# A hybrid encoder block on one core: four small changes to when background transfers and side work happen

## The chip, the cores and the metric

One Trainium2 chip, one of its cores. The metric is the time of one execution in device microseconds. A kernel is run several times; the median is compared.

## The reference, cut to what matters

One encoder layer on x (512 tokens, width 2048), all in float32:

```
h = rms_norm(x) ; proj = h @ w_in
  group A: 16 heads of chunked banded softmax attention with a relative bias
  group B: 4 heads of gated linear attention, RMSNorm per head, silu gate
x = x + concat(A, B) @ w_out
u = causal_conv3(rms_norm(x) @ w_ffn_up)         # 11264 columns
x = x + (gelu(u_gate) * u_val) @ w_ffn_down      # 5632 -> 2048
x = x + sigmoid(rms_norm(x) @ w_ple_gate) * (p @ w_ple_proj)
return rms_norm(x)
```

## The kernel before

**Arithmetic.** Activations lie transposed: features on the 128 partitions, 512 tokens in the free dimension. Every float32 product is made as three products of two parts: ScalarE copies an operand to its rounded high part (`hi`), VectorE subtracts to get the low part (`lo`), and TensorE does hi·hi, hi·lo and lo·hi. On top of that each large matrix product is done by a seven-product scheme on 2 x 2 blocks (Strassen-Winograd). The weight side needs the quarters L11, L12, L22 and four sums of quarters, S1 = L21 + L22, S2 = S1 + L11, S3 = L21 + L11, S4 = S2 + L12. The activation side needs seven operands, R11, R21, R22, N1, T3, N2, T4, made from four quarters of a pair of feature blocks.

**Units, steps, stages.** A unit is one block of output features; for each unit the seven products P1, P2, P6, P5, P7, P3, P4 run in this order, and one product of one unit is a *step*. The list `steps` runs over all stages in turn; `base[unit]` is the unit's first step. The first and the last two units of the later stages are interleaved, product by product (the *head* pair and the *last* pair). The stages:

- linear (units 16, 20/21, 17, 22/23, 18, 8, 9, 19; steps 0 to 69). 16 to 19 are the four heads of group B, 20 to 23 the values of group A in two pairs (14 steps each), 8 and 9 the first two blocks of the output gate;
- front (units 0 to 7, which are group A's heads by pairs, then the gate blocks 10 and 11; from step 70);
- embed: four steps, the product p @ w_ple_proj, 24 wide matmuls each; its results are evicted from PSUM by ScalarE (`pp_o`) and stored to memory (`ppd`) from ScalarE's queue;
- wo (out projection), up, dn0, dn1, dn2 (down projection in three chunks), pg (the embedding's gate).

**The main loop** goes over `steps`. `agenda[i]` is a list of (k, function) that are called at step i beside its product: those with k = 0 first, then the high part of the weight operand of step i + 2, then k = 1, then the low part, then the product, then those with k above 1. Instructions on TensorE, VectorE and ScalarE keep this order. DMA instructions do not: the framework orders each issuing queue (SP's, ScalarE's, GpSimd's) by a simulated run in which an instruction goes out once what it needs is ready. Only a DMA wrapped in `tc.keep_in_program_order` stays behind everything that was written for its queue before it. Once the order is fixed, a queue is strictly in order: an instruction that waits holds up all behind it.

**Weights.** A raw quarter is loaded by SP into a page of 128 x 1024 floats from a pool of free pages (`issue`, L429 for quarters `l`); S1 and S3 come as a load on SP (L433) and an accumulating DMA on GpSimd (L434) into the same page, both called `s` in the profile. A page is free again when its low part has been made.

**Sums in memory.** For the first two units of up, dn0, dn2 and pg all four sums are made in device memory instead (`memory_sums`, the kind `mem`): eight DMAs, memory to memory, of 512 KB (up), in this order: S1 = L21 (SP, L381), S1 += L22 (GpSimd, L384), S3 = L21 (SP), S2 = S1 (SP), S2 += L11, S3 += L11 (GpSimd), S4 = S2 (SP), S4 += L12 (GpSimd). In the profile those of up's two units are called `up0S` and `up8S`. `MEMORY` (L1140) says at which steps they are issued: for up from step 12 on, one each 6 steps (the two units one after the other, to step 102); for the others from the first step of the fifth unit of up on, one each 5 steps.

**The output gate.** A gate unit u = 8 + g multiplies silu(r) with a head's normed output `on`, which `load_heads` (L882, DMA at L885) loads into a page of ring `x` at step base + 3 (g = 0), 6, 3, 6. In linear and front the ring `x` has one page only; the value units' results (`vo`, stored to `vad`, L1083) and `tp` use the same one. Then `store_pair` (L266) makes the other operands N1, T3, N2, T4 in a `tp` page and stores all seven to memory, R11, R21 and R22 straight from the unit's own page `u` (`mix_R`), N and T from `tp` (`mix_N`, `mix_T`); all these DMAs are SP's (L264). The ring `u` has two pages there. Of gate block 11 nothing is stored: its operands stay in SBUF (`tails[1]`).

**Splits for wo.** The operands of wo are loaded and split from the end of front on; the last two feature blocks come from `tails` by `wo.split(op, 1, False, (0,))` and `(1,)`. For `(1,)` the steps are i0 + 8, 9, 10, 12, 15, 14, 15 in the order of the products, with i0 the base of unit 11: i0 + 7 to i0 + 10 are the embedding's four blocks, and the first step of wo is i0 + 11.

**Squares.** For the next RMSNorm, `squares` makes ScalarE square a unit's two halves into one buffer `sq`, and VectorE add each to `acc`. `after_norm` (wo and dn2) calls it from the third step after the unit's last one.

Of the kernel before, what the change touches and what calls it, by code (L numbers as in the profile page):

```python
# [43 lines left out]
def encoder_block(ctx: ExitStack, tc: tile.TileContext, A, out):  # L44
    nc = tc.nc
# [54 lines left out]
    def page(ring, name, dt=F32, shape=(P, 1024)):  # L100
        tags = rings[ring]
        i = counts.get(ring, 0)
        counts[ring] = i + 1
        tag = tags[i % len(tags)]
        return page_pool(tag).tile(list(shape), dt, tag=tag, name=name)
# [152 lines left out]
    def operand_scratch(name, kb):  # L258
        n = (min(4, kb), kb - 4)
        return {(op, g): dp.tile([P, n[g] * 256], F32, name=f"{name}_{op}{g}") for op in OPS for g in range(2)}  # L260

    def store_operand(xd, op, k, src):
        c = k % 4 * 256
        nc.sync.dma_start(xd[op, k // 4][:, c:c + 256], src)  # L264

    def store_pair(xd, k, a, b, t=None):  # L266

        t = (page("x", "tp") if t is None else t).rearrange("p (o t) -> p o t", o=4)
        a0, a1, b0, b1 = a[:, 0:256], a[:, 256:512], b[:, 0:256], b[:, 256:512]
        ops = dict(R11=a0, R21=b0, R22=b1, N1=t[:, 0, :], T3=t[:, 1, :], N2=t[:, 2, :], T4=t[:, 3, :])  # L270

        def store(*names):
            for op in names if xd else ():
                store_operand(xd, op, k, ops[op])

        store("R11", "R21", "R22")
        vec.tensor_tensor(ops["N1"], a0, a1, ALU.subtract)
        store("N1")
        vec.tensor_tensor(ops["T3"], b1, a1, ALU.subtract)
        store("T3")  # L280
        vec.scalar_tensor_tensor(ops["N2"], ops["N1"], -1.0, b1, ALU.mult, ALU.subtract)
        store("N2")
        vec.scalar_tensor_tensor(ops["T4"], ops["N2"], -1.0, b0, ALU.mult, ALU.subtract)
        store("T4")
        return ops
# [3 lines left out]
    def xtile(op, g, name, dt=F32R):  # L289
        pool = xa[0] if X_TAGS.index((op, g)) < 6 else xb[0]  # L290
        return pool.tile([P, 2, 1024], dt, tag=f"{op}{g}", name=name)

    mixd = operand_scratch("mix", 8)
# [79 lines left out]
    def memory_sums(unit):  # L373
        n = unit.stage.kb * P
        w = lambda q: unit.stage.weights(unit.u, q)
        for q in ("S1", "S2", "S3", "S4"):
            in_memory[unit, q] = dp.tile([P, n], F32, name=f"{unit.stage.name}{unit.u}{q}")
        S = lambda q: in_memory[unit, q]

        def first(q, src):  # L380
            tc.keep_in_program_order(nc.sync.dma_start(S(q), src, max_dma_last_dim=n))  # L381

        def added(q, src):
            tc.keep_in_program_order(nc.gpsimd.dma_start(S(q), src, accum_op=ALU.add, max_dma_last_dim=n))  # L384

        return [lambda: first("S1", w("L21")), lambda: added("S1", w("L22")), lambda: first("S3", w("L21")),
                lambda: first("S2", S("S1")), lambda: added("S2", w("L11")), lambda: added("S3", w("L11")),
                lambda: first("S4", S("S2")), lambda: added("S4", w("L12"))]
# [217 lines left out]
    def load_x(src, unit):  # L606
        unit.xs = page("c", "xs").rearrange("p (s t) -> p s t", s=2)
        nc.sync.dma_start(unit.xs, src[unit.u])

    def residual(dst, unit):  # L610
        vec.tensor_tensor(unit.xs, unit.o, unit.xs, ALU.add)
        nc.sync.dma_start(dst[unit.u], unit.xs)

    def squares(unit, at, c=slice(0, T)):

        def square(s):
            if unit.first and s == 0:
                act.activation(acc[:, c], unit.xs[:, s, c], AF.Square)
            else:
                sqt[unit, s] = tp.tile([P, T], F32, tag="sq", name="sq")[:, c]  # L620
                act.activation(sqt[unit, s], unit.xs[:, s, c], AF.Square)

        def add(s):
            if (unit, s) in sqt:
                vec.tensor_tensor(acc[:, c], acc[:, c], sqt[unit, s], ALU.add)

        return [(at + i, k, lambda f=f, s=s: f(s)) for i, k, f, s in ((0, 2, square, 0), (1, 1, add, 0), (1, 2, square, 1),
                                                                      (2, 1, add, 1))]
# [3 lines left out]
    def weighted(col, unit):  # L632
        m = unit.u
        for s in range(2):
            act.activation(unit.o[:, s, :], unit.xs[:, s, :], AF.Copy, scale=col[:, m + 8 * s:m + 8 * s + 1])
# [29 lines left out]
    def after_norm(dst, xd, col):  # L665
        def after(unit):
            if unit.last is not None:
                return [(1, 0, lambda: nc.sync.dma_start(dst[unit.u], unit.xs))] + squares(unit, 6 + unit.last * 2)
            return [(0, 1, lambda: residual(dst, unit)), (1, 2, lambda: weighted(col, unit)),
                    (2, 1, lambda: store_pair(xd, unit.u, unit.o[:, 0, :], unit.o[:, 1, :]))] + squares(unit, 3)  # L670
        return after

    def after_add(dst):
# [5 lines left out]
    def after_up(unit):  # L679
# [19 lines left out]
        def join():  # L699
            ci, k, second = unit.slot  # L700
            if second:
                store_pair(gd[ci], k, held[0], unit.c[:, 1, :])
            else:
                held[0] = unit.c[:, 1, :]
# [14 lines left out]
    def after_gate(unit):  # L719
# [9 lines left out]
    stages = [Stage("wo", list(range(8)), 8, mixd, blk2(A["w_out"]), after_norm(streams[1], h2d, nffn), "s3", "dma",  # L729
                    begin=lambda u: load_x(streams[0], u), begin_at=6, chained=True)]  # L730
# [151 lines left out]
    def load_heads(unit):  # L882
        g = unit.u - 8
        unit.M = {"on": page("x" if g < 3 else "c", "on").rearrange("p (s t) -> p s t", s=2)}
        nc.sync.dma_start(unit.M["on"], ond[g])  # L885

    def after_gates(unit):
        g, M = unit.u - 8, unit.M

        def times():  # L890
            vec.tensor_tensor(unit.o, unit.o, M["on"], ALU.mult)

        def pair():
            ops = store_pair(mixd if g < 3 else None, 3 + g, unit.o[:, 0, :], unit.o[:, 1, :])
            if g == 3:
                tails[1] = ops

        return [(0, 1, lambda: vec.tensor_tensor(unit.o, unit.o, rb2, ALU.mult)),
                (1 if g < 2 else 0, 1.5, lambda: act.activation(unit.o, unit.o, AF.Silu))] + (
                    [(4, 1, times), (5, 1, pair)] if g < 2 else [(1, 1, times), (1, 3, pair)] if g == 2 else  # L900
                    [(0, 3, times), (0, 4, pair)])
# [201 lines left out]
    front = Stage("in", [0, 1, 2, 3, 4, 5, 6, 7, 10, 11], 8, None, front_weights, front_after, "dma", "dma", single=True)  # L1103
# [26 lines left out]
    base = {}  # L1130
# [6 lines left out]
            need = [[(u, name) for name in (NEEDS[u.sums] if u.kind != "pp" else ("L11",))] for u in group]  # L1137
            wanted += [e for es in zip(*need) for e in es]

    MEMORY = ((lambda: 12, 6, (4,)), (lambda: base[stages[4].units[4]], 5, (5, 7, 8)))  # L1140
    agenda = [[] for _ in range(len(steps) + 60)]
    now = [0]
    for a, b in zip(stages[3:], stages[4:]):
        i0 = base[a.units[-1]]
        for n, p in enumerate(PLAIN):
            op = PRODUCTS[p][1]
            for g in range(2):
# [3 lines left out]
                at = 2 * n + (11 if g else 8)  # L1151
                if g and b.chained and op in ("R21", "T4"):
                    at = max(at, 14 if op == "R21" else 15)
# [3 lines left out]
    for st in (linear, front):  # L1157
        for u in st.units:
            if 16 <= u.u < 20:
                items = gla_head(u)  # L1160
                u.follow = lambda unit, items=items: items
                u.early()
            elif 8 <= u.u < 12:
                agenda[base[u] + (3, 6, 3, 6)[u.u - 8]].append((0, lambda u=u: load_heads(u)))

    i0 = base[front.units[-1]]
    for n, p in enumerate(PLAIN):
        op = PRODUCTS[p][1]
        for g in range(2):
            kept = (op, g) == ("T3", 1)  # L1170
            agenda[i0 + (13 if kept else n + 1 + g)].append((0, lambda op=op, g=g: wo.load(op, g)))
            agenda[i0 + (15 if kept else n + 5)].append((3, lambda op=op, g=g: wo.split(op, g, True, ())))
        at = (7, 7, 8, 9, 15, 10, 11)[n]
        agenda[i0 + at].append((3.5, lambda op=op: wo.split(op, 1, False, (0,))))
        at, k = ((8, 1), (9, 1), (10, 1), (12, 1), (15, 3.6), (14, 3), (15, 3.6))[n]
        agenda[i0 + at].append((k, lambda op=op: wo.split(op, 1, False, (1,))))

    def embedding_load(raw):
# [22 lines left out]
        aux_tags[:] = ["b6", "b7"]  # L1201
        banks.extend(("b4", "b5"))

    for b0, gap, heads in MEMORY:
        ops = [[op for u in stages[h].units[:2] for op in memory_sums(u)] for h in heads]
        for n, op in enumerate(sum(ops, [])):
            agenda[b0() + n * gap].append((0, op))

    agenda[base[front.units[7]] + 7 + 12].append((5, attention_done))
# [174 lines left out]
    for i, (unit, prod) in enumerate(steps[:-4]):  # L1384
# [17 lines left out]
        if i - len(steps) in EARLY:  # L1402
            p, op, g = EARLY[i - len(steps)]
            t = xtile(op, g, "last")
# [162 lines left out]
```

## Time and profile before

| | |
|---|---|
| median of 3 runs | 2234.06 us (2233.76 to 2234.48) |
| the profiled execution | 2231.0 us, span 2229.3 us, mean granted TensorE clock 0.994 |
| TensorE (PE) busy | 2192.5 us, 98% of the span |
| its weight loads (PEld) | 2146.3 us, 96%, beside the matmuls |
| VectorE (DVE) | 1905.9 us, 85% |
| ScalarE (ACT) | 1340.0 us, 60% |
| GpSimd (POOL) | 179.8 us, 8% |
| DMA | 550.83 MB, mean 247 GB/s |

How to read the rows of the trace: start in us from the span's start, duration in us, engine, line, operation, output<-inputs, count; in square brackets the idle time of the engine before it and what ended it. Nearly all lines read L64, since one wrapper issues them; go by tile names. SPq is SP's queue of DMA instructions: its duration is that of the issue and not of the transfer. `wsplit` is a weight operand's high and low part, `accA`, `accB`, `accC` are PSUM banks of the products, `u` is where a unit's result is gathered, `pat`, `eb`, `en`, `dd`, `pz` belong to a head of group B. Rows of waits: engine, what waited, for whom, us in total, times, longest. Rows of windows: the stretch, its length, then busy us and count of PE, PEld, DVE, ACT and POOL, the granted clock (1.00 is full), the DMA engines' busy share, GB/s. Rows of DMA: issues, size, median us from issue to landing.

### The profile page before, as it was taken

How to read it: one execution, taken by the hardware profiler on the slowest of the kernel's cores; microseconds unless marked ns; L12 is line 12 of the kernel's file. 1: busy time of each engine (PE TensorE's matmuls, PEld its weight loads, DVE VectorE, ACT ScalarE, POOL GpSimd, SP SyncE). 2: the span in 40 equal slices, each digit the busy share in tenths (PEclk: the TensorE clock that was granted, in tenths of full speed). 3: DMA queues.
4: the chain of work that ended last, by engine and by line, in shares of the span. 5: the costliest groups of instructions: out<-in, count | busy, mean ns of one | idle time of the engine just before them, and what ended most of it. 6: DMA issues, size and time to landing. Idle time of an engine off the chain costs nothing.

```text
span 2229.3 us, 46370 instructions
## 1 busy us (share of the span) xinstructions
PE 2192.5 (98%) x18588; PEld 2146.3 (96%) x18588; DVE 1905.9 (85%) x2616; ACT 1340.0 (60%) x2005; POOL 179.8 (8%) x212
## 2 busy tenths in 40 slices
PE   9999999999989999999999999999999999999997
PEld 7899899999989999999999999999999999999996
DVE  8476668999879898999889888888899798898987
ACT  9455455777765575555555555555574564666765
POOL 0010110000000001111111111111000100000000
PEclk9999999999999999999999999999999999999998
DMA  7478878876898988999999999998876977879996
GB/s 235 140 192 216 227 201 211 198 208 171 262 300 255 297 276 212 263 279 253 262 254 240 256 245 274 249 258 227 241 275 222 301 234 238 328 251 341 300 288 201
DMA packets 224553, 550.83 MB, mean 247 GB/s; under 512 B 21296, under 2 KB 100400, under 8 KB 224336
## 3 DMA queue, kind: packets, MB, share of 16 engines
q1 hardware_dynamic: 180560, 441.15, 57.2%
q0 software_dynamic: 40512, 101.46, 26.2%
q10 hardware_dynamic: 3264, 5.24, 0.6%
q8 instruction: 146, 2.39, 0.4%
q14 instruction: 71, 0.58, 0.1%
HBM read 474.37 MB, written 103.81 MB: 259 GB/s over the span
## 4 chain that ended last, share of the span: by engine, by line
PE 89%; DVE 6%; DMA 2%; ACT 2%; issue 1%; SPq 0%; ACTq 0%; DVEq 0%; POOLq 0%
PE accA L64 45%; PE accC L64 23%; PE accB L64 11%; DVE wsplit L64 2%; PE v L242 1%; PE v L243 1%; PE v L244 1%; PE py L64 1%; PE ptr L64 1%; PE psc L64 1%; DMA ppd<-pp_o 1%; DMA s<-in_w_blk 1%; PE pat L64 1%; PE po L64 1%; DVE u L64 1%
## 5 line engine op out<-in xcount | busy, mean ns | idle before, releaser
L64 DVE TENSOR_TENSOR wsplit<-l,wsplit 128x1024 fp32r<-128x1024 f32 (+1 forms) x462 | 554.8, 1202 | 119.2 <-ACT wsplit L64 118.5
L64 ACT ACTIVATE wsplit<-l 128x1024 fp32r<-128x1024 f32 (+1 forms) x462 | 481.2, 1042 | 280.6 <-PE accC L64 118.5
L64 DVE TENSOR_TENSOR wsplit<-s,wsplit 128x1024 fp32r<-128x1024 f32 (+1 forms) x267 | 320.3, 1201 | 69.9 <-ACT wsplit L64 69.5
L64 ACT ACTIVATE wsplit<-s 128x1024 fp32r<-128x1024 f32 (+1 forms) x267 | 277.1, 1038 | 59.1 <-PE accB L64 36.2
L64 ACT ACTIVATE u<-accA 128x256 f32<-128x256 f32 x302 | 114.3, 378 | 286.6 <-PE accA L64 277.3
L64 PE MATMUL accA<-up_T,wsplit 128*128 128x256 f32 x2112 | 253.3, 276 | 0.0
L64 PEld LDWEIGHTS accA<-up_T,wsplit 128*128 128x128 f32 x2112 | 245.7, 188 | 0.1
L64 DVE SCALAR_TENSOR_TENSOR cv<-u,cw,cv 128x511 f32<-128x511 f32 (+1 forms) x176 | 131.7, 748 | 3.1
L434 POOL DMA_DIRECT2D s<-in_w_up x84 | 74.4, 886 | 733.3 <-DMA s<-in_w_up 229.7
L64 PE MATMUL accA<-up_R,wsplit 128*128 128x256 f32 x1056 | 126.9, 276 | 0.0
L64 PE MATMUL accB<-up_R,wsplit 128*128 128x256 f32 x1056 | 126.5, 276 | 0.0
L64 PE MATMUL accC<-up_R,wsplit 128*128 128x256 f32 x1056 | 126.5, 276 | 0.0
L64 PE MATMUL accA<-up_N,wsplit 128*128 128x256 f32 x1056 | 126.5, 276 | 0.0
L64 PE MATMUL accC<-up_N,wsplit 128*128 128x256 f32 x1056 | 126.5, 276 | 0.0
L64 PE MATMUL accA<-dn_T,wsplit 128*128 128x256 f32 x1056 | 125.6, 276 | 0.2 <-DVE u L64 0.2
L64 PEld LDWEIGHTS accA<-up_R,wsplit 128*128 128x128 f32 x1056 | 122.9, 188 | 0.5 <-issue 0.5
L64 PEld LDWEIGHTS accB<-up_R,wsplit 128*128 128x128 f32 x1056 | 122.8, 188 | 0.0
L64 PEld LDWEIGHTS accC<-up_N,wsplit 128*128 128x128 f32 x1056 | 122.8, 188 | 0.0
L64 PEld LDWEIGHTS accA<-up_N,wsplit 128*128 128x128 f32 x1056 | 122.8, 188 | 0.0
L64 PEld LDWEIGHTS accC<-up_R,wsplit 128*128 128x128 f32 x1056 | 122.8, 188 | 0.0
L64 PEld LDWEIGHTS accA<-dn_T,wsplit 128*128 128x128 f32 x1056 | 122.4, 188 | 0.4 <-issue 0.4
L64 PE MATMUL accA<-in_T,wsplit 128*128 128x256 f32 x768 | 94.5, 279 | 2.4 <-ACT u L64 1.8
(345 smaller groups left out, 4235.7 us busy)
## 6 DMA issues: line engine op xcount, KB each, us to landing
l<-in_w_up SPq DMA_DIRECT2D x132, 512.0 KB, 5.4
s<-in_w_up SPq DMA_DIRECT2D x84, 512.0 KB, 5.3
s<-in_w_up POOLq DMA_DIRECT2D x84, 512.0 KB, 6.5
l<-in_w_dn SPq DMA_DIRECT2D x56, 448.0 KB, 5.6
l<-in_w_blk SPq DMA_DIRECT2D x48, 512.0 KB, 5.5
s<-in_w_blk SPq DMA_DIRECT2D x32, 512.0 KB, 4.5
s<-in_w_blk POOLq DMA_DIRECT2D x32, 512.0 KB, 7.4
l<-in_w_out SPq DMA_DIRECT2D x28, 512.0 KB, 5.1
```

The source lines that it names most:

```text
L64: ins = f(*args, **kw)
L242: nc.tensor.matmul(ps[t], x[:, 0, sl], wh, start=kt == 0, stop=False)
L243: nc.tensor.matmul(ps[t], x[:, 0, sl], wl, start=False, stop=False)
L244: nc.tensor.matmul(ps[t], x[:, 1, sl], wh, start=False, stop=kt == KD - 1)
L434: nc.gpsimd.dma_start(t, src("L22" if name == "S1" else "L11"), accum_op=ALU.add)
```

## The change

1. **Sums in memory.** Each unit has its own start and spacing. Up's first unit: from step 3, one each 4 steps (to step 31). Up's second unit: from the first step of front unit 1 (step 77), one each 5 steps (to 112). The 48 operations of dn0, dn2 and pg stay at the steps they had.
2. **Stores of the gate units.** For gate blocks 8 and 9 the stores of R11, R21 and R22 go on GpSimd's queue; those of N1, T3, N2 and T4 stay on SP's. `load_heads` of block 8 is called at step base + 5 instead of base + 3.
3. **Last pair's splits.** The three splits of `tails[1]` for the first three products come at i0 + 9, 10, 11 instead of i0 + 8, 9, 10.
4. **Squares.** For the second unit of a head pair (wo and dn2) they start one step later.

```diff
-    def store_operand(xd, op, k, src):
+    def store_operand(xd, op, k, src, queue=None):
         c = k % 4 * 256
-        nc.sync.dma_start(xd[op, k // 4][:, c:c + 256], src)
+        (queue or nc.sync).dma_start(xd[op, k // 4][:, c:c + 256], src)
...
-                store_operand(xd, op, k, ops[op])
+                store_operand(xd, op, k, ops[op], queue if op[0] == "R" else None)
...
-                    (2, 1, lambda: store_pair(xd, unit.u, unit.o[:, 0, :], unit.o[:, 1, :]))] + squares(unit, 3)
+                    (2, 1, lambda: store_pair(xd, unit.u, unit.o[:, 0, :], unit.o[:, 1, :]))] + squares(unit, 3 + (unit.head == 1))
...
-            ops = store_pair(mixd if g < 3 else None, 3 + g, unit.o[:, 0, :], unit.o[:, 1, :])
+            ops = store_pair(mixd if g < 3 else None, 3 + g, unit.o[:, 0, :], unit.o[:, 1, :], queue=nc.gpsimd if g < 2 else None)
...
-    MEMORY = ((lambda: 12, 6, (4,)), (lambda: base[stages[4].units[4]], 5, (5, 7, 8)))
+    MEMORY = [[(4, 0), lambda: 3, 4], [(4, 1), lambda: base[front.units[1]], 5]]
+    for n, (h, k) in enumerate(((5, 0), (5, 1), (7, 0), (7, 1), (8, 0), (8, 1))):
+        MEMORY.append([(h, k), lambda n=n: base[stages[4].units[4]] + 40 * n, 5])
...
-                agenda[base[u] + (3, 6, 3, 6)[u.u - 8]].append((0, lambda u=u: load_heads(u)))
+                agenda[base[u] + (5, 6, 3, 6)[u.u - 8]].append((0, lambda u=u: load_heads(u)))
...
-        at, k = ((8, 1), (9, 1), (10, 1), (12, 1), (15, 3.6), (14, 3), (15, 3.6))[n]
+        at, k = ((9, 1), (10, 1), (11, 1), (12, 1), (15, 3.6), (14, 3), (15, 3.6))[n]
...
-    for b0, gap, heads in MEMORY:
-        ops = [[op for u in stages[h].units[:2] for op in memory_sums(u)] for h in heads]
-        for n, op in enumerate(sum(ops, [])):
+    for (h, k), b0, gap in MEMORY:
+        for n, op in enumerate(memory_sums(stages[h].units[k])):
             agenda[b0() + n * gap].append((0, op))
```

More of the change, by code (lines that the diff above doesn't have):

```diff
@@ L260, in operand_scratch, with store_pair @@
         return {(op, g): dp.tile([P, n[g] * 256], F32, name=f"{name}_{op}{g}") for op in OPS for g in range(2)}
-    def store_operand(xd, op, k, src):
+    def store_operand(xd, op, k, src, queue=None):
         c = k % 4 * 256
-        nc.sync.dma_start(xd[op, k // 4][:, c:c + 256], src)
-    def store_pair(xd, k, a, b, t=None):
+        (queue or nc.sync).dma_start(xd[op, k // 4][:, c:c + 256], src)
+    def store_pair(xd, k, a, b, t=None, queue=None):
         t = (page("x", "tp") if t is None else t).rearrange("p (o t) -> p o t", o=4)
```

## The prediction

> **What bounds the kernel now.** First the page's busy shares, then TensorE's waits, then stretches of 40 us to find where it idles.
>
> ```profile
> PE 2192.5 (98%) x18588; PEld 2146.3 (96%) x18588; DVE 1905.9 (85%) x2616; ACT 1340.0 (60%) x2005; POOL 179.8 (8%) x212
> PE pp L64 <- ACT pp_o L64: 3.8, 1, 3.8
> PE accC L64 <- ACT u L64: 0.9, 1, 0.9
> 240.00:280.00 40.00, 35.33 (x263) 32.61 (x262) 23.27 (x28) 18.80 (x27) 3.68 (x5) 0.87 0.83 224
> 320.00:360.00 40.00, 35.82 (x295) 34.18 (x295) 29.22 (x39) 22.67 (x31) 4.55 (x5) 1.00 0.90 242
> ```
>
> TensorE is busy 2192.5 of 2229.3 us, and the change removes no matmul. What can be gained is its 36.8 us of idle time and whatever matmuls lose at a lowered clock. In 240 to 280 it idles 4.67 us and its mean granted clock is 0.87 (the last columns are clock, DMA share and GB/s); in 320 to 360 it idles 4.18 us at full clock. The wait of 3.8 us is in the embedding stage, the one of 0.9 us in the last down stage. I take these four places in turn, since each lies beside an edit.
>
> **Place A, 226 to 296 us: unit 18 and unit 8, the edit to the sums in memory.**
>
> ```profile
> 231.63 1.40 POOL L384 DMA_DIRECT2D up0S<-in_w_up  x1
> up0S<-in_w_up POOLq DMA_DIRECT2D x4, 512.0 KB, 13.9
> q0 software_dynamic: 1239, 1.67, 53.4%
> vad<-vo SPq DMA_DIRECT2D x8, 256.0 KB, 9.1
> SPq L885 <- DMA vad<-vo: 13.1, 2, 12.2
> 249.05 0.33 SPq L885 DMA_DIRECT2D on<-ond  x1
> 250.51 1.74 SPq L433 DMA_DIRECT2D s<-in_w_blk  x2
> 256.36 8.34 DMA s<-in_w_blk
> 264.79 1.22 DVE L64 TENSOR_TENSOR l<-l,s 128x1024 f32<-128x1024 f32 x1 [5.58 <-DMA s<-in_w_blk]
> 260.21 2.88 PE L64 MATMUL accA<-in_R,wsplit 128*128 128x256 f32 x24
> 267.28 1.46 PE L64 MATMUL accB<-in_R,wsplit 128*128 128x256 f32 x8 [2.38 <-DVE wsplit L64]
> 271.04 0.77 PE L64 MATMUL pat<-eb,en 128*128 128x128 f32 x2 [2.30 <-DVE eb L64]
> 271.00:275.60 4.60, 4.56 (x17) 3.23 (x17) 3.63 (x4) 0.00 (x0) 0.00 (x0) 0.50 0.44 130
> 295.94 3.30 PE L64 MATMUL accA<-in_R,wsplit 128*128 128x256 f32 x24
> ```
>
> Read it backwards. TensorE waits 2.38 us for a weight split and 2.30 us for `eb`; both stand on VectorE behind `l<-l,s`, which waited 5.58 us for an `s` load. That load's second half, GpSimd's accumulation, was issued at 256.36 and took 8.34 us; its first half left SP only at 250.51, because SP stood 12.2 us at `load_heads` (L885), whose page was still being read by a `vad` store. That store was in flight together with an accumulation for the up stage (231.63, the kind that takes 13.9 us to land), and GpSimd's queue took 53.4% of the DMA time in 232 to 250. After the change unit 0's eight operations are at steps 3 to 31 and unit 1's start at step 77, so nothing of this kind is left from step 32 to 76.
>
> The price: the 7 products from 260.21 to 295.94 took 35.73 us.
>
> ```profile
> 340.16 2.88 PE L64 MATMUL accA<-in_R,wsplit 128*128 128x256 f32 x24
> 368.08 3.30 PE L64 MATMUL accA<-in_R,wsplit 128*128 128x256 f32 x24
> ```
>
> The same work around the next head, 340.16 to 368.08, took 27.92 us, of which place B counts 0.5 as a wait: 27.4 clean. A loses 35.73 - 27.4 = 8.3 us: 4.7 of waits, the rest matmuls at a granted clock of 0.50 in 271.00 to 275.60. By the Trainium skill, page "TensorE: Matmul & The Clock Gate", part 1, the clock halves after an idle window of about 3.4 us. Neither wait here is that long alone, so read per wait it would grant no clock loss and A would be worth 4.7; the row of 0.50 decides, and I keep 8.3.
>
> Does the wait go entirely? For that, `s` must land 4.7 us before 256.36 + 8.34 = 264.7, by 260.0. SP reached `load_heads` at 249.05 - 12.2 = 236.9, just after the store, which so took 12.2 us or more. At the median of 9.1 (a median with such accumulations beside it) SP is free 3 us sooner, and the 8.34 us may shrink by 1 (estimate): 0.7 us of wait would be left, at full clock. With a store faster than that median nothing is left. So 7 to 8.3 us; I take 7.5. Moving `load_heads(8)` from step base+3 to base+5 I cost at nothing: at 249 us TensorE is at step 45, seven steps short of its place in the program, so its page sets its time and not its step; should it come behind the `s` loads, A only gets safer.
>
> **Place B, 308 to 350 us: unit 19, the stores on GpSimd's queue.**
>
> ```profile
> 239.91 2.89 PE L64 MATMUL accA<-in_R,wsplit 128*128 128x256 f32 x24
> 308.80 1.74 SPq L381 DMA_DIRECT2D up8S<-in_w_up  x1
> 311.40 1.67 SPq L264 DMA_DIRECT2D mix_R<-u  x3
> 315.39 2.88 PE L64 MATMUL accA<-in_R,wsplit 128*128 128x256 f32 x24
> 323.06 0.38 ACT L64 ACTIVATE u<-accA 128x256 f32<-128x256 f32 x1 [6.14 <-DMA mix_R<-u]
> 330.91 0.86 POOL L434 DMA_DIRECT2D s<-in_w_blk  x1 [21.43 <-DMA s<-in_w_blk]
> 345.60 0.39 ACT L64 ACTIVATE u<-accA 128x256 f32<-128x256 f32 x1 [3.17 <-DMA mix_R<-u]
> ```
>
> Unit 19's first eviction needs the `u` page that unit 8's three R stores still read. They leave SP from 311.40 behind a copy for the up stage (308.80), and ScalarE stands until 323.06, 6.14 us, with the next weight split behind it. Unit 19 lasts 340.16 - 315.39 = 24.77 us; the same seven products and `pz` of unit 18 take 260.21 - 239.91 = 20.30. That is 4.5 us, and 0.5 more at the next head's `pat` (the 3.17 us wait on unit 9's stores): 5.0 in all. After the change the copy is gone from SP, and the stores go on GpSimd, which idles 21.43 us before 330.91. Three issues at 0.86 us add 2.6 us to GpSimd, where no accumulation stands behind them until 330.91; the N and T stores on SP go 1.67 us earlier. Issued by 312, they land at 318 to 320 if they take 6 to 8 us (323.06 - 313.07 = 10 on SP); the eviction's product ends at 315.39 + 2.88 = 318.3. So 3.5 to 5.0 are gained; I take 4.2.
>
> The rule against it: page "DMA: Bandwidth & Descriptors" of the Trainium skill, section "Issuing engines are not separate DMA queues", says that transfers from any engine run on the same 16 DMA engines and that another issuer saves only issue time. By it the landing would stay at some 10 us; no run here shows yet which holds. That is a rival below.
>
> **Place D, embedding, 606 to 634 us: the last pair's splits.**
>
> ```profile
> 606.71 11.07 PE L64 MATMUL pp<-ps,wsplit 128*128 128x512 f32 x48
> 620.60 0.42 ACT L64 ACTIVATE wo_R<-u 128x256 fp32r<-128x256 f32 x1 [1.81 <-DVE u L64]
> 621.56 12.84 PE L64 MATMUL pp<-ps,wsplit 128*128 128x512 f32 x48 [3.78 <-ACT pp_o L64]
> 630.75 1.09 ACT L64 ACTIVATE pp_o<-pp 128x512 f32<-128x512 f32 x2 [1.92 <-DMA ppd<-pp_o]
> 634.24 5.62 PE L64 MATMUL accA<-wo_R,wsplit 128*128 128x256 f32 x48
> ```
>
> Half the work takes 11.07 us, all of it 27.53 (606.71 to 634.24): 5.4 lost. ScalarE stands 1.81 us at the R11 split of the last pair, then splits 0.42 us, before it evicts for the second block; with the split one block later these evictions start 2.2 us sooner. What is late next: the page that `ppd` still reads, which stops ScalarE at 630.75 whatever comes before, and ScalarE's full load as the out projection begins, where three splits now come one step nearer their use. Bounds 0 and 5.4 (if the clock stays up too); I take 1.5, nearer the 2.2 less that second stop.
>
> **Place E, second down-stage head: the squares.**
>
> ```profile
> 1961.98 0.63 ACT L64 ACTIVATE sq<-xs 128x512 f32<-128x512 f32 x1 [2.54 <-DVE acc L64]
> ```
>
> Two squares share one buffer, the second waits 2.54 us for VectorE's sum, and an eviction behind it costs TensorE the 0.9 us of the second row of waits above. A step later the buffer is free: 0.9 gained, bounds 0 and 1. The same edit in the out projection meets no wait of TensorE: 0.
>
> **What it adds: eight sums in steps 3 to 31.**
>
> ```profile
> 118.14 0.88 POOL L434 DMA_DIRECT2D s<-in_w_v_a  x1 [16.52 <-DMA s<-in_w_v_a]
> 126.86 1.23 DVE L64 TENSOR_TENSOR l<-l,s 128x1024 f32<-128x1024 f32 x1 [0.17 <-DMA s<-in_w_v_a]
> 129.56 0.46 PE L64 MATMUL pat<-eb,en 128*128 128x128 f32 x2
> 157.58 0.86 POOL L434 DMA_DIRECT2D s<-in_w_blk  x1 [17.71 <-DMA s<-in_w_blk]
> q1 hardware_dynamic: 180560, 441.15, 57.2%
> q0 software_dynamic: 40512, 101.46, 26.2%
> ```
>
> By the last two rows 0.52 MB costs the 16 DMA engines 1.5 us on q1 (57.2% of 2229.3 us over 441.15 MB) and 3.0 us on q0. The first copy, at step 3 (about 113 us), goes on SP just ahead of the loads that GpSimd waits for at 118.14. VectorE already waits 0.17 us for their sum at 126.86, and `pat` follows at 129.56 with hardly any slack: 1.5 us of delay can pass straight to TensorE. The next head's loads meet an extra accumulation of 3.0 us. Bounds 0 and 3.0 (twice 1.5); I take 1.5. On SP the copy S2<-S1 now follows the accumulation into S1 by 8 steps instead of 12; at 2.9 us a step (20.30 / 7) that is 23 us, against 13.9 to land, so 0, but see the second rival. Unit 1's eight operations, at steps 77 to 112, lie under attention, where TensorE waits for no load: 0. The other stages' 48 operations keep their steps.
>
> Sum: 7.5 + 4.2 + 1.5 + 0.9 - 1.5 = 12.6 us. The profiled execution took 2231.0 us (span 2229.3 and 1.7 around it), so 2218.4; the median of the runs is 3.06 above it: 2221.5, called 2222.
>
> **Rivals.** (1) The queue does not matter, as the skill's rule has it: only the copy that left SP (1.5 us) and 1.7 us of issue help, B gives 1.5: 2234.1 - 9.9 = 2224. For it: DMA share 0.90 in 320 to 360; against it: SP's queue holds loads ahead of the stores, GpSimd's does not. Chance 0.15.
> (2) Slower: S2<-S1 stands on SP waiting for the accumulation into S1, as `load_heads` does now. Place: step 15, about 151 us (`pat` at 129.56 is in step 9). It decides if that accumulation is queued on GpSimd behind the one of 157.58, which waits for unit 17's loads, so that it lands near 172: SP stands 21 us, and unit 17's second sum comes that late less the few us it has to spare, 18, with some 3.5 of lowered clock as in A. Less the 14.1 gained: +7, 2241. Chance 0.08.
> (3) The store before `load_heads` lands late without the sums too, A stays: gain 5.1, 2229. For it: the weight loads of that stretch and their own accumulations stay. Chance 0.14.
> (4) The loads of both early heads come so late that each `pat` wait trips the clock: 2 x 5.6 instead of 1.5, gain 3: 2231. Chance 0.07.
>
> **How the numbers follow.** The forecast has 0.56, at 2222. About 0.2% (4.5 us) is what a measurement of this kernel can tell from none. Faster: 0.56 + 0.15 + half of (3) = 0.77; same: half of (3) and (4), 0.14; slower, with (2) and a little for what I don't see: 0.09. Range: low end 2215.5, with A 8.3, B 5.0, D 4, E 1 and no cost (18.3); high end 2231, which takes in (3) and (4) and leaves out (2).
>
> **What would show it.** A: SP's wait at `load_heads` under 8 us, no TensorE wait between 250 and 285, clock 1.00 there. B: ScalarE's wait for `mix_R` under 2 us. D: TensorE's wait at `pp` near 1.6 us, perhaps a second one. E: no wait of accC for ACT. Cost: a new wait at `pat` near 130 and one head later. The forecast is wrong if TensorE idles anew between 100 and 240, or if A's wait stays.

## The result, and the profile after

| | before | after |
|---|---|---|
| median of 6 runs each, same chip | 2234.73 us | 2224.57 us (2221.58 to 2225.85) |
| ratio | | 0.995 [0.9939, 0.996] |
| profiled execution | 2231.0 us, span 2229.3 | 2225.11 us, span 2223.4 |
| mean granted clock | 0.994 | 0.997 |

The change gains 10.2 us by the medians; 12 were forecast. The page of the changed kernel, then its longest waits of TensorE beside the edits, then the two stretches of 40 us that the prediction began with (columns as there):

```profile
PE 2188.4 (98%) x18588; PEld 2141.1 (96%) x18588; DVE 1905.3 (86%) x2616; ACT 1339.5 (60%) x2005; POOL 182.9 (8%) x218
```

```profile
PE pp L64 <- ACT pp_o L64: 3.9, 3, 2.0
PE pat L64 <- DVE eb L64: 2.4, 3, 1.4
PE accA L64 <- ACT u L64: 2.2, 2, 1.9
```

```profile
240.00:280.00 40.00, 40.00 (x332) 38.20 (x331) 28.72 (x35) 21.99 (x32) 3.49 (x4) 1.00 0.81 217
320.00:360.00 40.00, 37.07 (x309) 35.62 (x308) 30.83 (x41) 21.82 (x31) 5.22 (x7) 1.00 0.71 187
```

Place A is clean: 40 of 40 us busy at full clock. Place B is not: 2.9 us idle are left. From the timeline, SP's waits and the loads of place A:

```profile
236.79 1.11 SPq L1083 DMA_DIRECT2D vad<-vo  x2
244.14 0.33 SPq L885 DMA_DIRECT2D on<-ond  x1
252.26 0.89 POOL L434 DMA_DIRECT2D s<-in_w_blk  x1 [18.29 <-DMA s<-in_w_blk]
262.03 2.88 PE L64 MATMUL accA<-in_R,wsplit 128*128 128x256 f32 x24
289.21 1.03 PE L64 MATMUL accA<-in_R,wsplit 128*128 128x256 f32 x4
```

```profile
SPq L885 <- DMA vad<-vo: 6.2, 1, 6.2
```

```profile
vad<-vo SPq DMA_DIRECT2D x4, 256.0 KB, 5.6
```

SP still stands at load_heads, in its old place in the queue, but 6.2 us instead of 12.2, since the `vad` stores land in 5.6 us; the same answer for before (226 to 262 us) has them at 8.9, beside two accumulations for the up stage of 15.3. From unit 8's first product to unit 9's are 27.18 us instead of 35.73.

**One profile is not enough here.** Each row of the next table is one execution; a cell is the difference of the start times of two first products (`accA<-in_R`, for the embedding `pp<-ps`) in its timeline. "Linear" goes from unit 16's at 103.35 to unit 18's at 239.91 (times of before), "unit 8" from 260.21 to 295.94, "B" from unit 19's to front unit 1's, 315.39 to 368.08, "attention" from there to the embedding, 606.71, "embedding" to the out projection's third unit, 675.25, "rest" to the end of the span. The last column is VectorE's wait for `s` loads under attention. The rows other than before and after are the experiments below.

| execution | linear | unit 8 | B | attention | embedding | rest | `s` waits |
|---|---|---|---|---|---|---|---|
| before | 136.56 | 35.73 | 52.69 | 238.63 | 68.54 | 1554.05 | 1.1 |
| before again | 137.68 | 36.96 | 53.15 | 241.08 | 69.46 | 1553.87 | 5.5 |
| sums as before | 138.62 | 36.61 | 52.89 | 240.32 | 67.93 | 1553.62 | 4.6 |
| sums only | 141.57 | 27.18 | 51.66 | 239.84 | 69.42 | 1553.76 | 2.3 |
| after | 138.46 | 27.18 | 51.80 | 242.15 | 67.87 | 1552.91 | 6.1 |
| load_heads as before | 137.30 | 27.18 | 51.75 | 242.24 | 67.95 | 1553.91 | 6.6 |
| stores on SP | 137.80 | 27.18 | 51.53 | 242.88 | 67.62 | 1552.61 | 7.2 |
| second unit in wo | 137.16 | 27.18 | 51.24 | 242.81 | 68.01 | 1555.22 | 7.1 |
| sums under attention | 137.27 | 27.18 | 50.84 | 243.53 | 68.55 | 1552.82 | 7.8 |
| stores from tp | 137.84 | 27.18 | 48.08 | 241.59 | 68.08 | 1552.85 | 4.5 |
| third page | 136.81 | 27.18 | 48.76 | 238.69 | 68.23 | 1552.78 | 0.2 |
| S1 first | 137.81 | 27.18 | 51.60 | 238.54 | 68.58 | 1553.39 | 0 |
| both | 140.97 | 27.16 | 48.25 | 238.58 | 67.94 | 1552.88 | 0 |
| both, linear too | 136.16 | 27.18 | 47.94 | 238.59 | 68.10 | 1553.19 | 0.8 |

### The profile page after: what moved, and what is told of

It is laid out like the page before. It is cut to its first block, busy times and chain, and to the rows that moved or that the text cites. A ratio compares the mean times of both kernels' runs of the same rounds, so it can differ in the third digit from the quotient of the medians.

```text
span 2223.4 us, 46366 instructions
## 1 busy us (share of the span) xinstructions
PE 2188.4 (98%) x18588; PEld 2141.1 (96%) x18588; DVE 1905.3 (86%) x2616; ACT 1339.5 (60%) x2005; POOL 182.9 (8%) x218
## 4 chain that ended last, share of the span: by engine, by line
PE 81%; DVE 9%; DMA 5%; ACT 2%; issue 2%; POOL 0%; ACTq 0%; DVEq 0%; SPq 0%; POOLq 0%
PE accA L64 42%; PE accC L64 21%; PE accB L64 11%; DVE wsplit L64 2%; DMA s<-in_w_blk 2%; PE v L244 1%; PE v L242 1%; PE v L243 1%; DVE sc L64 1%; DVE u L64 1%; DMA s<-in_w_v_a 1%; DVE s L64 1%; ACT wsplit L64 1%; PE po L64 1%; PE ptr L64 1%
```

## Experiments

All start from the changed kernel, unless said otherwise; ratios are to the kernel before, run beside them.

**1. Sums only** (the kernel before with part 1). Diff: the hunks on `MEMORY` and its loop.

> The kernel before with part 1 alone (both units' sums at their new steps). Theory, from the two traces: place A gains 8.5 (no wait of TensorE between 240 and 300), the two `pat` waits cost 1.9, place B gains 0.9 at most because a copy leaves SP, and 3.5 are lost between 380 and 605, since the second unit's sums move under attention. Sum about -4: 2230 to 2231 against some 2234.7. Rival: the 3.5 lost under attention are not the sums' doing; then -7.5, 2227. As I predicted it blind: -7.5 (A), +1.5 (early cost), -1.5 (B), 2227 too, but with no new waits under attention.

2225.2 us, 0.9963 [0.9951, 0.9975]: 8.6 us of the 10 are part 1's. The theory's 4 falls; the rival's 7.5 is near. Unit 8 takes 27.18 us. Attention lost nothing against the three executions with the old sums (239.84; they took 238.63 to 241.08), with 2.3 us of `s` waits. Linear took 141.57 us, 5 more than in the first profile of before, and here is why: the timeline has the wait at the second `pat`, and the window behind it the mean granted clock, 0.61.

```profile
200.08 0.46 PE L64 MATMUL pat<-eb,en 128*128 128x128 f32 x2 [1.39 <-DVE eb L64]
203.51 5.30 PE L64 MATMUL accB<-wsplit,in_R 128*128 128x256 f32 x24
```

```profile
200.00:207.50 7.50, 7.42 (x34) 6.39 (x35) 5.23 (x6) 0.51 (x1) 0.71 (x1) 0.61 0.70 123
```

The changed kernel's own trace, with a wait as long, keeps its clock in the same window:

```profile
129.86 0.46 PE L64 MATMUL pat<-eb,en 128*128 128x128 f32 x2 [0.48 <-DVE eb L64]
199.56 0.46 PE L64 MATMUL pat<-eb,en 128*128 128x128 f32 x2 [1.41 <-DVE eb L64]
```

```profile
200.00:207.50 7.50, 7.50 (x60) 6.87 (x60) 5.61 (x7) 1.55 (x2) 1.03 (x1) 1.00 0.68 129
```

So in these two executions a wait of 1.4 us cost 1.4, or 1.4 + 7.5 x 0.39 = 4.3.

**2. Sums as before** (part 1 undone).

```diff
-    MEMORY = [[(4, 0), lambda: 3, 4], [(4, 1), lambda: base[front.units[1]], 5]]
...
+    MEMORY = ((lambda: 12, 6, (4,)), (lambda: base[stages[4].units[4]], 5, (5, 7, 8)))
```

> The changed kernel with part 1 undone: sums at the steps they had, the other three parts stay. Theory: the embedding's splits give 1.0 and the squares 0.95, the stores on GpSimd nothing that can be seen: 2232 to 2233, and A's two waits with the granted clock near 0.5 stand at 267 and 271 as before. As predicted blind: 1.5 + 0.9 + 2.7 of B that I gave to the queue itself: 2229.6.

2233.56 us, 0.9998 [0.9989, 1.0006]: the other three parts together don't show in the time. The interval runs from 2.5 us gained to 1.3 lost, so a gain of 2 us is not excluded either. The two waits of place A are back, with the clock:

```profile
269.90 1.19 PE L64 MATMUL accB<-in_R,wsplit 128*128 128x256 f32 x8 [2.93 <-DVE wsplit L64]
273.66 0.77 PE L64 MATMUL pat<-eb,en 128*128 128x128 f32 x2 [2.57 <-DVE eb L64]
```

```profile
270.00:277.50 7.50, 4.93 (x22) 3.73 (x22) 7.21 (x9) 2.07 (x3) 0.00 (x0) 0.59 0.22 68
```

Its place B is instructive. The copy for the up stage is still on SP here, the stores are on GpSimd, and ScalarE's waits for the stores of unit 8 and then of unit 9 are 2.44 and 6.54 us, where before has 6.14 and 3.17:

```profile
312.76 1.65 POOL L264 DMA_DIRECT2D mix_R<-u  x3
323.44 0.38 ACT L64 ACTIVATE u<-accA 128x256 f32<-128x256 f32 x1 [2.44 <-DMA mix_R<-u]
349.34 0.38 ACT L64 ACTIVATE u<-accA 128x256 f32<-128x256 f32 x1 [6.54 <-DMA mix_R<-u]
```

So unit 19 was 2.6 us shorter (22.20 against 24.77), and front unit 0 took 30.69 us instead of 27.92; nothing was left.

**3. Stores on SP.**

```diff
-... queue=nc.gpsimd if g < 2 else None)
+... queue=None)
```

> The changed kernel with the R stores of gate blocks 8 and 9 on SP's queue again (the rest of the change stays). Theory (the queue does not matter, only what is in flight): the three stores of block 8 land some 11 us after issue on either queue, ScalarE waits 5 to 6 us for them, time within 1 us of the changed kernel, 2224 to 2226. Rival, my blind forecast: the queue itself is worth 2.7 of B's 4.2, so 2227 and a wait above 7 us; and unit 9's stores wait 3 us again.

2222.14 us, 0.995 [0.9938, 0.9962]; B takes 51.53 us against 51.80. With the copy gone, the queue makes no difference. First the stores and the loads ahead of them in the changed kernel (loads on SP, stores on GpSimd), then all on SP:

```profile
300.47 3.74 SPq L429 DMA_DIRECT2D l<-in_w_blk  x3
303.13 1.65 POOL L264 DMA_DIRECT2D mix_R<-u  x3
315.45 0.38 ACT L64 ACTIVATE u<-accA 128x256 f32<-128x256 f32 x1 [5.26 <-DMA mix_R<-u]
```

```profile
l<-in_w_blk SPq DMA_DIRECT2D x3, 512.0 KB, 10.0
mix_R<-u POOLq DMA_DIRECT2D x3, 128.0 KB, 11.2
```

```profile
302.16 3.74 SPq L429 DMA_DIRECT2D l<-in_w_blk  x3
305.94 1.80 SPq L264 DMA_DIRECT2D mix_R<-u  x3
316.74 0.38 ACT L64 ACTIVATE u<-accA 128x256 f32<-128x256 f32 x1 [4.85 <-DMA mix_R<-u]
```

```profile
mix_R<-u SPq DMA_DIRECT2D x3, 128.0 KB, 9.6
```

GpSimd issued the stores 2.66 us after the burst of three 512 KB loads began, SP 3.78 us after. ScalarE went on 15.0 and 14.6 us after that beginning. The three stores of unit 9 are of the same size, but one load instead of three goes out just ahead of them (at 327.02 and 328.31), and they land in about half the time on either queue. First in the changed kernel, then with all on SP:

```profile
mix_R<-u POOLq DMA_DIRECT2D x3, 128.0 KB, 5.9
```

```profile
mix_R<-u SPq DMA_DIRECT2D x3, 128.0 KB, 5.6
```

So the time to landing goes with the loads ahead of the stores and not with who issues them. No run takes the burst itself away.

**4. Second unit in wo.**

```diff
-... [(4, 1), lambda: base[front.units[1]], 5]]
+... [(4, 1), lambda: base[wo.units[0]] + 2, 4]]
```

> The changed kernel with the second unit's eight sums moved from steps 77 to 112 (under attention) to the out projection: from its first step plus 2, one each 4 steps. Theory: the 3.5 us between 380 and 605 come back, 2221, and the waits of TensorE for `PT` and `sc` there are gone. Rival 1: those 3.5 differ from run to run and have nothing to do with the sums: 2224.6, and waits under attention of about 1 us stay. Rival 2: the out projection, where TensorE is busy 40 of 40 us and the DMA share is 0.74 to 1.00, pays instead: some 2224 to 2228 with new waits after 640.

2224.18 us, 0.9954 [0.9942, 0.9966]. My theory fell: without any sum under attention the stretch still took 242.81 us, with 7.1 us of `s` waits. Rival 2 shows a little too: the rest took 1555.2, some 2 us more than in the others.

**5. load_heads as before**, base + 3.

```diff
-... (5, 6, 3, 6)[u.u - 8] ...
+... (3, 6, 3, 6)[u.u - 8] ...
```

> The changed kernel with load_heads of block 8 called at its old step, base + 3. Its instructions stand in the same order on every engine and queue, so it is also a second look at the changed kernel. Theory: 2222 to 2226, unit 8 again 27.2 us long (262.03 to 289.21 in the changed kernel), and whatever differs between its trace and that of the changed kernel is what differs from one execution to the next: above all the stretch from front unit 1 to the embedding, 242.15 us in the changed kernel, 238.63 before, 239.8 to 242.9 in the four runs since. Rival: the two steps matter, SP stands at load_heads longer than 6 us again and unit 8 takes over 28 us.

2224.14 us, 0.9955 [0.9941, 0.997]; unit 8 again 27.18. SP stands 6.3 us at load_heads. The move is worth nothing, as costed. As a second look it repeats every stretch of the changed kernel within 0.1 us, but for linear and the rest (1.2 less, 1.0 more).

**6. Before again.** No edit.

> The kernel before, unchanged, profiled a second time. Theory: its first profiled execution was a lucky one (3.7 us under the median of its runs), and the 3.5 us that the changed kernel seems to lose under attention are that luck: now front unit 1 to the embedding takes some 240 to 241 us instead of 238.63, VectorE waits 4 us or more in all for `s` loads there instead of 1.1, and the stretch from unit 17 to unit 18 (68.27) takes 69 to 70 as it did with the same sums in the second run of this study. Rival: both stretches are 238.6 and 68.3 again; then the changed kernel really loses 3.5 us under attention and 1.4 at its second head.

One profile, 2237.36 us. VectorE's waits under attention in the first profile of before, and in this one:

```profile
DVE s L64 <- DMA s<-in_w_blk: 1.1, 2, 0.8
```

```profile
DVE s L64 <- DMA s<-in_w_blk: 5.5, 5, 1.7
```

The first execution was a lucky one by 2.5 us under attention and 1.1 in linear. Still, 241.08 is less than the 241.59 to 243.53 of six of the eight executions with part 1 and the loads' order unchanged; the other two have 239.84 and 238.69.

**7. Sums under attention** (both units').

```diff
-... [[(4, 0), lambda: 3, 4], [(4, 1), lambda: base[front.units[1]], 5]]
+... [[(4, 0), lambda: base[front.units[0]] + 1, 4], [(4, 1), lambda: base[front.units[0]] + 33, 4]]
```

> The changed kernel with the sums of both units under attention: steps 71 to 99 and 103 to 131, one each 4 steps; none is left in the linear stage. Theory: the waits at the two `pat` come with the loads of the stage itself (the second one was there with the sums at their old steps too, 1.69 us), so the linear stage is no faster by more than 0.5 us, attention takes 242 as it did, time 2223 to 2226. Rival 1, my blind costing of the early sums at 1.5: the two `pat` waits shrink under 0.2 each and the time is 2222.5. Rival 2: eight more sums under attention delay the `s` loads there and it loses 2 or more.

2224.26 us, 0.9957 [0.9944, 0.997]. Linear took 137.27 us with no sum in it; with the early sums and the same loads it took 136.8 to 138.5 where the clock held. The early sums cost less than 1 us there. Attention took 243.53, the longest of all and 1.4 more than in the changed kernel, but the median does not show it (2224.57 there).

**8. Stores from tp.**

```diff
+                if queue and k == 3 and op[0] == "R":
+                    continue
                 store_operand(xd, op, k, ops[op], queue if op[0] == "R" else None)
+                if queue and k == 3 and op != "T4":
+                    store_operand(xd, dict(N1="R11", T3="R21", N2="R22")[op], k, ops[op], queue)
```

> Place B by itself. The three stores of gate block 8 that read the page `u` are made from `tp` instead (N1, T3 and N2 go where R11, R21 and R22 belong, so the operands of the out projection are not the right ones): the same traffic at nearly the same time on the same queue, but unit 19's first eviction no longer waits for a store. Theory (the landing of the stores is what holds unit 19, and the load burst ahead of them sets it): ScalarE's wait of 5.3 us is gone, unit 19 takes 20.3 to 21 us instead of 23.88, and the time falls by about 3, to 2221.5. Rival: the `s` and `l` loads of the same burst land as late and hold unit 19 or the next head instead, which lasted 30.69 us in the run where unit 19 took only 22.20; then the time stays at 2224.

2221.98 us, 0.995 [0.9936, 0.9964], against 2224.14 and 2224.26 of its neighbours. Unit 19 now runs through:

```profile
308.60 2.88 PE L64 MATMUL accA<-in_R,wsplit 128*128 128x256 f32 x24
311.52 0.38 ACT L64 ACTIVATE u<-accA 128x256 f32<-128x256 f32 x1 [1.38 <-PE accA L64]
328.89 2.88 PE L64 MATMUL accA<-in_R,wsplit 128*128 128x256 f32 x24
```

20.29 us, with no wait for a store. So 3.6 us of unit 19 were left, all of them that wait. By the medians 2.2 of them reach the end; the intervals overlap.

**9. Third page**, the same with nothing left out.

```diff
-            unit.o = page("u", "u").rearrange("p (s t) -> p s t", s=2)
+            own = page("u", "u") if (unit.stage.name, unit.u) != ("in", 19) else pg.tile([P, 1024], F32, tag="c0", name="u")
+            counts["u"] += (unit.stage.name, unit.u) == ("in", 19)
+            unit.o = own.rearrange("p (s t) -> p s t", s=2)
...
-    agenda[base[linear.units[-1]]].append((0, lambda: retire("c0")))
+    agenda[base[linear.units[-1]] - 6].append((0, lambda: retire("c0")))
```

> The changed kernel with a third page for unit 19's result: it takes c0, which is withdrawn from the weight pages six steps earlier for it, so its first eviction waits for no store and nothing is left out. Theory (the landing of block 8's stores is all that is left of place B): unit 19 takes 20.3 to 21 us instead of 23.88, and the time falls by 3, to 2221. Rival: with one weight page less for six steps some loads come later, and unit 9 or unit 19 waits for a weight split instead; then 2224 or more.

2220.31 us, 0.9941 [0.9928, 0.9953]. Unit 19 takes 20.81 us. Its profile also has hardly an `s` wait under attention (0.2), and 238.69 us there: not expected.

**10. S1 first.**

```diff
-... NEEDS[u.sums] if u.kind != "pp" ...
+... (("L11", "S1", "L12", "S2*", "S3", "L22") if u.stage is front else NEEDS[u.sums]) if u.kind != "pp" ...
```

> The changed kernel with one order of loads turned round in the front stage: S1 of each unit is asked for ahead of L12, so that its accumulation lands some 1.5 us sooner and L12 as much later. Theory: TensorE's loss under attention (242.15 us from front unit 1 to the embedding, against 238.63 in the first profile of the kernel before) is VectorE's waiting for the `s` loads handed on, about 0.7 us for each us that it waits (1.13 us of such waits gave 238.63, 5.49 gave 241.08, 7.81 gave 243.52): the waits fall from 6 to under 2 us, the stretch to 239 to 240, the time to 2221.5. Rival 1: these waits are a symptom of VectorE running ahead and cost nothing: they vanish and the stretch stays at 242. Rival 2: L12 comes too late, TensorE waits for its split at accB, and the time is 2226 or more.

2221.48 us, 0.9946 [0.9934, 0.9959]. In one head of the changed kernel, S1's load, its accumulation, the sum and a wait of TensorE behind it:

```profile
559.22 3.17 SPq L433 DMA_DIRECT2D s<-in_w_blk  x2
564.38 0.87 POOL L434 DMA_DIRECT2D s<-in_w_blk  x1 [23.54 <-DMA s<-in_w_blk]
571.86 1.23 DVE L64 TENSOR_TENSOR s<-s,l 128x1024 f32<-128x1024 f32 x1 [0.79 <-DMA s<-in_w_blk]
583.21 1.57 PE L64 MATMUL py<-PT,va 128*64 128x128 f32 x16 [0.95 <-ACT PT L64]
```

The same head with S1 first:

```profile
554.18 0.33 SPq L433 DMA_DIRECT2D s<-in_w_blk  x1
558.14 0.87 POOL L434 DMA_DIRECT2D s<-in_w_blk  x1 [16.87 <-DMA s<-in_w_blk]
568.20 1.22 DVE L64 TENSOR_TENSOR s<-s,l 128x1024 f32<-128x1024 f32 x1
```

The accumulation goes out 10.1 us ahead of the sum instead of 7.5. No `s` wait is left, the wait at `py` is gone, and the stretch takes 238.54 us. Rival 1 falls: the waits are paid for, and rival 2 does not show. The stretch says so, and it is as short in the two runs below that keep this order (238.58, 238.59); the time alone would not, since its interval overlaps that of the changed kernel.

**11. Both.** Diffs 9 and 10.

> The third page and S1 ahead of L12 in the front stage together. Theory: they lie at different places, so their gains add: 3 + 2.5, 2219. Rival: whatever unit 19 gains is given back under attention, since VectorE and the loads there don't come sooner: 2221.5.

2218.5 us, 0.9934 [0.9922, 0.9947], near the theory's 2219. The gains of the two runs before, 4.3 and 3.1 us by the medians, add in part: attention, 238.58 here, had been as short in the third page's profile (238.69). In its profile the second `pat` waits 1.57 us and the clock falls again, which is 3 us of linear's 140.97.

**12. Both, linear too.**

```diff
+... ("L11", "S1", "L12", "S3", "L22") if u.stage is linear else ...
```

> As the run before, and S1 ahead of L12 in the linear stage too, where the second head's `pat` waits for VectorE 0.55 to 1.7 us in every kernel so far behind an `s` load. Theory: both `pat` waits shrink to under 0.3 us, the linear stage to unit 18 gets 1 us shorter, 2218. Rival: in the linear stage L12 has no time to spare, and a wait of TensorE for its split takes their place: no gain or a loss of 1 to 3.

2215.9 us, 0.9922 [0.9909, 0.9936], the best of all. Its page, and what is left of the waits that the prediction spoke of:

```profile
PE 2186.9 (99%) x18588; PEld 2142.1 (97%) x18588; DVE 1904.9 (86%) x2616; ACT 1340.5 (61%) x2005; POOL 183.0 (8%) x218
```

```profile
PE pp L64 <- ACT pp_o L64: 4.0, 3, 2.1
```

```profile
100.00:240.00 140.00, 140.00 (x1160) 135.42 (x1160) 95.44 (x113) 75.19 (x103) 15.51 (x18) 1.00 0.82 216
```

Both `pat` waits of linear are gone, TensorE is busy 140 of 140 us at full clock, and no wait for L12 has come in their place. The wait at the embedding's `pp` is the longest that is left.

## Why the prediction was right, and where it was not

The terms, each as the mean over the executions of the table with and without the edit:

| term | forecast | found | from |
|---|---|---|---|
| A, unit 8 | +7.5 (7 to 8.3) | +9.2 | 36.43 (three with the old sums) to 27.18 |
| B | +4.2 (3.5 to 5.0) | +1.5 | 52.91 to 51.41 (after, runs 4, 5, 7) |
| D, embedding | +1.5 | +1.1 | 69.14 (three) to 68.08 (eleven) |
| E, squares | +0.9 | +0.8 | 1553.9 (three) to 1553.1 (ten, without run 4) |
| early sums | -1.5 | -0.8 | 137.62 to 138.41 (nine), two of them with the clock down; the other seven have 137.60 |
| attention | 0 | -1.7 | 240.01 to 241.72 (after, runs 1, 3, 4, 5, 7, 8, 9) |
| sum | 12.6 | 10.1 | the medians differ by 10.2 |

**A** was read rightly, backwards from TensorE's wait over VectorE, the `s` load, SP at load_heads to the `vad` store and the accumulation beside it. Its signs came: SP's wait at load_heads 6.2 us, no wait of TensorE there, the clock at 1.00; and run 2, with the sums back, has the waits and the lowered clock again. Only its upper bound was too low: the clean stretch is 27.18 us and not 27.4, and the bound was made from one execution, where with the old sums the other two lost 0.9 and 1.2 us more.

**B is the step that failed.** Its sign did not come: ScalarE's wait for `mix_R` is 5.26 us and not under 2. "They land at 318 to 320 if they take 6 to 8 us" took the landing for a property of the queue. The stores took 11.2 us on GpSimd and 9.6 on SP, and in the seven executions without the copy where unit 19 waits for them ScalarE went on 14.0 to 15.0 us after the burst of loads began, on either queue. The copy that left gives some 1.3 us (52.91 to 51.60 in runs 1 and 3), near the first rival's 1.5, and the queue next to nothing (51.41 on GpSimd, 51.60 on SP). Only where the copy stood ahead of the stores on SP (run 2) did GpSimd get them down sooner, 13.3 us after the burst's beginning instead of 15.9, and there the next head lost it again. The rule of the Trainium skill, page "DMA: Bandwidth & Descriptors", section "Issuing engines are not separate DMA queues", that I had weighed against the row and given 0.15, is borne out by run 3. What I should have seen is in the trace of before: three loads issued just ahead of the stores (311.40 in the prediction).

```profile
307.20 1.56 SPq L429 DMA_DIRECT2D l<-in_w_blk  x2
310.97 0.38 SPq L429 DMA_DIRECT2D l<-in_w_blk  x1
```

**D and E** came near the forecast. D's 1.1 is a difference of means and less sure: the first profile of before took 68.54, no longer than the longest with the edit (68.58). The one wait of 3.78 us at `pp` (two, of 4.2 in all, in the other executions without the edit) became three of 1.54, 0.34 and 1.98, no less in all; the last stands behind the page that `ppd` still reads, and the gain lies around them. E is sure: TensorE waits for nothing from 1900 to 2000 us, where it idled 0.95 us in all three executions without the edit.

**The early sums** cost half of what I took, and not in the way I took: without the two executions with the lowered clock nothing is left of the 0.8. By the prediction's last sentence new idling between 100 and 240 us would have made it wrong; what idling there is (0.48 and 1.41 us at the two `pat` of the changed kernel) is the cost that it foretold, and the old sums have such waits too. The second `pat` waited 0.81 and 1.69 us in two of three executions with the old sums, 0.39 to 1.57 us in the nine with the early ones; in two of these the clock fell as well: the fourth rival's mechanism, at one head, at 4.3 us by run 1 where it took 5.6 without a working. That the early sums are the cause of these two falls is not shown. The second rival (S2 behind S1 on SP) never showed: after the change that copy goes out at 154.35 without a wait.

**The loss under attention was costed at 0**, since "TensorE waits for no load" there. TensorE does not, but VectorE does. It is busy 77.84 of 82 us there (411 to 493 in before), and it hands on more than half of what it waits: a straight line through the fourteen rows of the table gives 238.3 us and 0.6 more for each us of its waits. 1.1 us of waits go with 238.63 us, 2.3 with 239.84, 4.5 to 5.5 with 240.3 to 241.6, 6 to 8 with 242.1 to 243.5, and 0 with 238.5, where run 10 took them away. That is shown. What makes the waits longer after the change is not, nor that the change does it every time (runs 1 and 9): not the second unit's sums (run 4), not the queue (run 3), and in run 9 they went without being aimed at. A VectorE that is late frees its pages late, so that the next load is late: such a lag would feed itself, and what starts it is open.

So luck helped the total: A came out 1.7 more than taken and the early sums 0.7 cheaper, against B's 2.7, attention's 1.7 and 0.5 of D and E that were not there. Two slips of the working change nothing: 0.56 + 0.15 + 0.07 is 0.78 and not 0.77, and 18.3 off the median gives 2215.8 and not 2215.5.

## What to carry over

An engine with 5% to spare beside TensorE hands a part of its waits on, here some 0.6 of each us: read its waits for loads too, before a stretch is called free. Moving a transfer to another queue changes when it is issued, which need not change when it lands; look at what was issued ahead of it on any queue, and rather give the waiting writer a page of its own. Of a term of 1 to 3 us, take two profiles: here two of one kernel differed by 6.4 us of span.

## What the runs showed that I had not expected

- The granted clock went to 0.50 (202 to 206 us) after single waits of 1.39 and 1.57 us (runs 1 and 11) and stayed at 1.00 after 1.41 (after) and 1.69 us (run 2), all at the same `pat`, with few matmuls around it; a fall costs some 3 us. The Trainium skill, page "TensorE: Matmul & The Clock Gate", part 1, speaks of a window of about 3.4 us that runs freely: that fits a fall that comes by chance, while the waits here are shorter than the idle window that it names. No run here shows such a window itself.
- Three stores of 128 KB took 9.6 to 11.2 us behind three loads of 512 KB, as long as these (10.0), and 5.6 to 5.9 us behind one.
